# Small 64-row products of two recurrent mixers, regrouped: heads alternate between the halves of the array

## The chip, the cores and the metric

The kernel runs on one core of one Trainium2 chip, in one launch. The metric is the device time of that launch in microseconds (us): the median of three runs of the kernel before is 1320.38 us (1319.36 to 1322.54). About 0.3% (4 us) is what a measurement of this kernel can tell from no change.

## The reference

One layer of a trunk with 256 positions and width 2048: a row norm, one wide projection, two recurrent mixers side by side, an output projection, and a gated feed-forward with its norm and the final norm.

```python
h = rms_norm(x, attn_norm_w);  proj = h @ w_in
y_a = rwkv7_mixer(proj[:, :N_RWKV_IN], ...)      # 16 heads of 64
y_b = gdn_mixer(proj[:, N_RWKV_IN:], ...)        # 8 value heads of 128, 4 key heads
x = x + concat([y_a, y_b]) @ w_out
h = rms_norm(x, ffn_norm_w)
x = x + (silu(h @ w_gate) * (h @ w_up)) @ w_down
out = rms_norm(x, final_norm_w)

# RWKV, one step:   S = S * w_t + (S a_t) b_t^T + v_t k_t^T;   y_t = S r_t
# delta rule, by chunks of 64:
v_new = u_i - w_i @ S                 # u, w: solutions of a unit triangular system of the chunk
o     = qg_i @ S + A_i @ v_new
S     = S * exp(gl_i) + kg_i^T @ v_new
```

Both recurrences are computed in chunks of 64 positions, four chunks for 256 positions. Within a chunk everything is a small matrix product (mostly 64 x 64 or 64 x 128), and the state goes from chunk to chunk.

## The kernel before, in words

**The stream.** Nearly all the work is the product of x (and later of y and of the feed-forward's activations) with weights that come once from memory. A block of weights (128 x 1024) is loaded on SyncE's queue into one of three raw buffers (L167), split by ScalarE into a high part (`wh`, L176) and by VectorE into a low part (`wl`, L177), and used by TensorE in `products` (L198, L199, L200: 128 x 128 weights, 256 columns, three products to a k-block; L195 and L196 in the feed-forward). I call these the stream products. Their result goes to the PSUM tag `pb`.

**The side work.** The mixers are Python generators (`prep`, `chain`, `gdn_v`, `gdn`). After every k-block of the stream `tick()` lets each generator emit its next step when its inputs are there. A scheduler then sets the final order on each engine, and TensorE works strictly through its order: a small product that waits holds the stream products behind it. Three PSUM tags of two banks each serve the side work: `mr` (preparation of RWKV), `mc` (its chain) and `mg` (delta rule).

**The shape of a small product.** The part of the array that a product uses follows from its operands: its rows are the partitions of the two inputs, its columns the partitions of the output. A product with inputs on partitions 0 to 63 and output on partitions 0 to 63 uses one quarter, one with all 128 input partitions and an output on partitions 64 to 127 one half of the columns. The products of full fp32 operands show in the trace as two MATMUL rows each (two passes), so 8 products are "x16" there. Transposes and the stream products show as one.

**RWKV.** Four head pairs p at a time (a half `hf` of the heads). Of the two heads h of a pair one lies on partitions 0 to 63 and one on 64 to 127 (`hr`).
- `prep` makes, per pair, `ps_A` (L464: four chunks for head 0 into one bank, then four for head 1 into another, each bank followed by a masking copy L466).
- `chain` first inverts the triangular blocks, then runs through the chunks: `psR` (L544; heads alternate between the column halves), `psU` (L552; one bank for each head, four pairs each, its copies L553 by ScalarE and by VectorE), `psS` (L561; heads alternate), and `psY`, the output: for each head, per pair, a product with the old state (L580, 64 x 64, not in the first chunk) and then at once one that adds the chunk's own part to it (L581, 128 rows x 64 columns), so the two kinds alternate. One ScalarE copy per head follows (L582).
- After the last chunk the gate: `ps_g`, per pair a product over 128 rows (L617) and one over the remaining 32 rows (L618) of the low-rank input `sgd1`, `sgd2`.

**Delta rule.** `gdn` makes decays and gates, inverts, and runs through four chunks, eight value heads each: `psK` (L856), `psUg` (L867, four heads to a bank, all on the same quarter of the array; copies L871, L873), `psSg` (L881), `psOg` (L895, four heads to a bank, one quarter; copy L896). At the end `ps_og` (L919) transposes the result, L920 scales it into `yg`.

**Where the mixers end.** The output projection multiplies first the half of `w_out` that goes with RWKV's output, then the half that goes with `yg`, which L221 and L222 have split into a high and a low part (`ys`). The delta rule's last chunks run beside the first half.

Of the kernel before, what the change touches and what calls it, by code (L numbers as in the profile page):

```python
# [17 lines left out]
P = 128  # L18
# [31 lines left out]
def trunk_kernel(ctx, tc, xT, vecs, fnw, w_up, a_up, g_up, w_in, w_ab, w_out, w_gu, w_dn, out):  # L50
# [30 lines left out]
    # times a head's rows: less their mean  # L81
    cmat = cp_.tile([P, P], F32, name="cmat")
    V.scalar_tensor_tensor(cmat, bones, -1.0 / 64, ident, ALU.mult, ALU.add)
    # cols 0..63: j < t, cols 64..127: j <= t, with j the partition modulo 64
# [26 lines left out]
    sgd2 = cp_.tile([32, T], F32, name="sgd2")  # L111
# [8 lines left out]
    def rsqrt(y, xh, tag):  # L120
        """1 / sqrt(2 xh) of a few columns of positive numbers: a guess by the exponent, then Newton's steps."""
# [59 lines left out]
    def proj(parts, wide=False, tag="pb"):  # L181
        """parts: [(weight source, rhs tiles)], each of 8 k-blocks of one block of 128 columns."""
        ps = pm.tile([P, 512], F32, tag=tag, name="psb")
        for j, (src, rhs) in enumerate(parts):
            products(ps, load_split(src), rhs, j == 0, j == len(parts) - 1, wide)
        return ps
# [18 lines left out]
    def evac_norm(ps):  # L205
        """an output block of the first projection, times the row norm, to the next of two padded tiles."""
# [29 lines left out]
    # the first blocks of columns: their products with a half of x, while the other comes  # L236
# [29 lines left out]
    # zero, but only when that part of x is split: the squares stand back for the splits  # L266
# [32 lines left out]
    sigmoid(sgd2, pl2[0:32, :])  # L299
# [7 lines left out]
    # 32 x 32 diagonal blocks by forward substitution, a block and every other column of it to a partition  # L307
# [67 lines left out]
    def prep(hf):  # L375
# [15 lines left out]
        for gr in range(2):  # L391
            key = (hf, gr)
            yield lambda: key in kt
            psw, psa = mps("ps_w", "mr"), mps("ps_a", "mr")
# [47 lines left out]
            for pi in range(2):  # L442
# [15 lines left out]
                yield None  # L458
                for h in range(2):
                    hr = slice(h * 64, h * 64 + 64)  # L460
                    ps = mps("ps_A", "mr")
                    ps3 = ps.rearrange("p (c f) -> p c f", c=NCH)
                    for ch in range(NCH):
                        PE.matmul(ps3[:, ch, :], bk[hr, ch].rearrange("p a t -> p (a t)"),  # L464
                                   ar[hr, p, ch].rearrange("p a t -> p (a t)"), start=True, stop=True)
                    V.tensor_tensor(AT[:, h, p], ps3, tmask[:, None, :].to_broadcast([P, NCH, P]), ALU.mult)  # L466
# [8 lines left out]
            # the rows of b make place for a, those of a for the inverse  # L475
# [27 lines left out]
    def chain(hf):  # L503
# [29 lines left out]
        # the output by positions: the norms run along its rows  # L533
# [4 lines left out]
        for ch in range(NCH):  # L538
# [7 lines left out]
            yield None  # L546
            for h in range(2):
                hr = slice(h * 64, h * 64 + 64)
                psU = mps("psU", "mc")
                U3 = psU[0:64, 0:256].rearrange("p (a f) -> p a f", a=4)  # L550
                for p in range(4):
                    PE.matmul(U3[:, p, :], ar[hr, p, ch, 0, :], RR[hr, p, :], start=True, stop=True)  # L552
                (S.copy, V.tensor_copy)[h](UV[0:64, ch, :, hr], U3)  # L553
# [19 lines left out]
            rows = slice(x * 64, x * 64 + 64)  # L573
# [614 lines left out]
```

## Time and profile before

| | |
|---|---|
| runs | 1322.54, 1319.36, 1320.38 us; median 1320.38 |
| span of the profiled execution | 1318.5 us, 1.9 us below the median |
| TensorE busy | 1300.2 us (99%) |
| VectorE busy | 933.2 us (71%) |
| ScalarE busy | 732.0 us (56%) |
| mean granted TensorE clock | 0.995 |
| first to last small product of the mixers (ps_w to ps_og) | 41.1 to about 516 us |
| feed-forward's stream (L195, first start) to the end | from 568.9 us |

The table is read so: TensorE has work nearly all the time. Matmuls overlap in the records (a stream product lasts 0.28 us in its row, but they start every 0.12 us), so what a product costs is seen from the starts of successive rows, not from the duration column.

### The profile page before, as it was taken

To read this page: it belongs to the slowest core of one execution; us is meant where nothing else is said; L and a number is where in the kernel's file an instruction comes from. 1 tells how busy PE (TensorE), PEld (TensorE's weight loads), DVE (VectorE), ACT (ScalarE), POOL (GpSimd) and SP (SyncE) were. 2 spreads that over 40 slices of the span, in tenths; PEclk is the share of its full clock that TensorE was granted. 3 is DMA by queue.
4 is the path that set the end of the run, shared out by engine and by line. 5 is a ranking of instruction groups with operands and counts; after the bars stand their busy time and mean duration, and the time that the engine had idled before them with its cause. 6 is when DMAs were issued, how large, how long until landed. Compare 5 with 4: busy or idle time off the path is not lost.

```text
span 1318.5 us, 23067 instructions
## 1 busy us (share of the span) xinstructions
PE 1300.2 (99%) x8458; PEld 1150.2 (87%) x8458; DVE 933.2 (71%) x1981; ACT 732.0 (56%) x1471; POOL 16.9 (1%) x63
## 2 busy tenths in 40 slices
PE   7999999999999999999999999999999999999997
PEld 7999999898889889998888888888888888888886
DVE  6987798678665667876776666676767676666764
ACT  6666656556644546666655454555555555555553
POOL 1000000000000000000000000000000000000000
PEclk9999999999989999999999999999999999999999
DMA  7454655445546234555765565555555555555541
GB/s 235 146 171 159 165 175 136 129 134 144 130 168 165 90 112 163 195 173 189 256 218 186 190 190 184 193 184 192 190 192 189 186 188 190 191 190 186 187 157 64
DMA packets 108129, 226.80 MB, mean 172 GB/s; under 512 B 52272, under 2 KB 54448, under 8 KB 107760
## 3 DMA queue, kind: packets, MB, share of 16 engines
q1 hardware_dynamic: 103744, 222.19, 53.6%
q10 hardware_dynamic: 4128, 2.10, 0.5%
q8 instruction: 66, 1.08, 0.3%
q0 software_dynamic: 144, 1.05, 0.2%
q14 instruction: 47, 0.39, 0.1%
HBM read 218.75 MB, written 4.46 MB: 169 GB/s over the span
## 4 chain that ended last, share of the span: by engine, by line
PE 96%; DVE 1%; DMA 1%; ACT 0%; issue 0%; SPq 0%; DVEq 0%; ACTq 0%
PE psb L195 25%; PE psd L1055 17%; PE psb L196 12%; PE psb L200 10%; PE psb L199 10%; PE psb L198 10%; PE psY L581 1%; PE ps_A L464 1%; PE psY L580 1%; PE psUg L867 1%; PE psOg L895 1%; DVE wl L177 1%; PE psd L1093 1%; PE psd L1091 1%; PE psd L1092 1%; DMA xraw<-in_xT 1%
## 5 line engine op out<-in xcount | busy, mean ns | idle before, releaser
L176 ACT ACTIVATE wh<-raw 128x512 fp32r<-128x512 f32 x780 | 489.4, 631 | 434.2 <-PE psb L195 139.1
L177 DVE TENSOR_TENSOR wl<-raw,wh 128x512 fp32r<-128x512 f32 x780 | 535.3, 690 | 272.3 <-ACT wh L176 268.3
L195 PE MATMUL psb<-x2s,wh 128*128 128x512 f32 x1408 | 497.4, 398 | 0.0
L196 PE MATMUL psb<-x2s,wl 128*128 128x256 f32 x1408 | 395.1, 282 | 0.7 <-DVE wl L177 0.7
L195 PEld LDWEIGHTS psb<-x2s,wh 128*128 128x128 f32 x1408 | 263.9, 188 | 63.5 <-ACT wh L176 0.2
L196 PEld LDWEIGHTS psb<-x2s,wl 128*128 128x128 f32 x1408 | 265.9, 189 | 3.6 <-DVE wl L177 1.5
L198 PE MATMUL psb<-xs,wh 128*128 128x256 f32 x816 | 236.9, 290 | 8.2 <-ACT wh L176 5.8
L200 PE MATMUL psb<-xs,wl 128*128 128x256 f32 x816 | 237.5, 291 | 0.5 <-DVE wl L177 0.5
L199 PE MATMUL psb<-xs,wh 128*128 128x256 f32 x816 | 237.3, 291 | 0.0
L1055 PE MATMUL psd<-wh,h 128*128 128x512 f32 x640 | 199.2, 389 | 0.0
L198 PEld LDWEIGHTS psb<-xs,wh 128*128 128x128 f32 x816 | 158.5, 194 | 11.5 <-ACT wh L176 5.8
L200 PEld LDWEIGHTS psb<-xs,wl 128*128 128x128 f32 x816 | 158.4, 194 | 5.8 <-issue 2.5
L199 PEld LDWEIGHTS psb<-xs,wh 128*128 128x128 f32 x816 | 158.5, 194 | 3.6 <-issue 1.9
L1055 PEld LDWEIGHTS psd<-wh,h 128*128 128x128 f32 x640 | 119.4, 188 | 24.9
L1055 PE MATMUL psd<-wl,h 128*128 128x512 f32 x320 | 124.4, 389 | 0.0
L200 PE MATMUL psb<-ys,wl 128*128 128x256 f32 x256 | 73.7, 288 | 0.0
L199 PE MATMUL psb<-ys,wh 128*128 128x256 f32 x256 | 73.6, 288 | 0.0
L198 PE MATMUL psb<-ys,wh 128*128 128x256 f32 x256 | 73.3, 286 | 0.0
L1055 PEld LDWEIGHTS psd<-wl,h 128*128 128x128 f32 x320 | 60.1, 188 | 12.5
L1061 DVE TENSOR_TENSOR acc<-acc,psd 128x512 f32<-128x512 f32 x80 | 51.2, 681 | 2.5 <-PE psd L1055 2.5
L200 PEld LDWEIGHTS psb<-ys,wl 128*128 128x128 f32 x256 | 49.0, 191 | 1.6 <-issue 1.5
L199 PEld LDWEIGHTS psb<-ys,wh 128*128 128x128 f32 x256 | 49.0, 191 | 1.5 <-issue 1.4
(315 smaller groups left out, 1152.2 us busy)
## 6 DMA issues: line engine op xcount, KB each, us to landing
raw<-in_w_gu SPq DMA_DIRECT2D x176, 512.0 KB, 3.5
raw<-in_w_in SPq DMA_DIRECT2D x99, 512.0 KB, 3.6
raw<-in_w_dn SPq DMA_DIRECT2D x80, 512.0 KB, 3.5
raw<-in_w_out SPq DMA_DIRECT2D x32, 512.0 KB, 3.6
raw_end<-in_w_dn SPq DMA_DIRECT2D x8, 512.0 KB, 3.9
xraw<-in_xT SPq DMA_DIRECT2D x8, 256.0 KB, 7.5
x<-in_xT SPq DMA_DIRECT2D x1, 2048.0 KB, 8.4
raw<-in_w_ab SPq DMA_DIRECT2D x2, 512.0 KB, 6.9
```

What stands on the lines that cost most here:

```text
L176: S.activation(wh, raw[:, hs], AF.Copy)
L177: V.tensor_tensor(wl, raw[:, hs], wh, ALU.subtract)
L195: PE.matmul(ps, wh[:, ks], rt[:, ri, :], start=st, stop=False)
L196: PE.matmul(ps[:, T:], wl[:, ks], rt[:, ri, 0:T], start=False, stop=sp)
L198: PE.matmul(ps[:, 0:T], wh[:, ks], rt[:, ri, 0:T], start=st, stop=False)
L199: PE.matmul(ps[:, 0:T], wh[:, ks], rt[:, ri, T:], start=False, stop=False)
L200: PE.matmul(ps[:, 0:T], wl[:, ks], rt[:, ri, 0:T], start=False, stop=sp)
L464: PE.matmul(ps3[:, ch, :], bk[hr, ch].rearrange("p a t -> p (a t)"), ar[hr, p, ch].rearrange("p a t -> p (a t)"), start=True, stop=True)
L580: PE.matmul(Y3[rows, p, :], ar[hr, p, ch, 1, :], St[hr, p, :], start=True, stop=False)
L581: PE.matmul(Y3[rows, p, :], AT[:, h, p, ch, 64:128], UV[:, ch, p, hr], start=(ch == 0), stop=True)
L1055: PE.matmul(banks[tb * 2 + cg], st, parts[cg][w], start=(i == 0 and w == 0 and st is hh), stop=(i == n - 1 and st is hl))
L1061: V.tensor_tensor(acc[:, tb, cs], acc[:, tb, cs], banks[tb * 2 + cg], ALU.add)
```

## The change

Seven edits; comments in the source were also dropped, which shifts line numbers by a few.

1. `ps_A`: the two heads' banks are opened together (one from `mr`, one from `mg`), and the products go chunk by chunk, heads alternating. Both masking copies follow the eight products.
2. `psU`: both heads write one bank, each on its own half of the partitions, heads alternating.
3. `psY`: first the eight products with the state, then the eight of the chunk, heads alternating between the halves. The output of a head stands on its own half of the partitions (before: on the half of the chunk's parity). One bank for both heads.
4. `psUg`: one bank for all eight value heads, even heads on partitions 0 to 63, odd ones on 64 to 127, alternating. Its readers take the even and the odd heads apart; VectorE's scaling now stands ahead of ScalarE's copy.
5. `psOg`: the same.
6. `sgd2` and the second part of the gate's weights are padded from 32 to 128 rows with zeros (two memsets on GpSimd), so both products of `ps_g` use all rows.
7. `ps_a` takes its bank from `mg` instead of `mr`.

```diff
-    sgd2 = cp_.tile([32, T], F32, name="sgd2")
+    sgd2 = cp_.tile([P, T], F32, name="sgd2")
+    G.memset(sgd2, 0.0)
...
-            psw, psa = mps("ps_w", "mr"), mps("ps_a", "mr")
+            psw, psa = mps("ps_w", "mr"), mps("ps_a", "mg")
...
+                psA = [mps("ps_A", tg).rearrange("p (c f) -> p c f", c=NCH) for tg in ("mr", "mg")]
+                for ch in range(NCH):
+                    for h in range(2):
+                        hr = slice(h * 64, h * 64 + 64)
+                        PE.matmul(psA[h][:, ch, :], bk[hr, ch].rearrange("p a t -> p (a t)"),
+                                   ar[hr, p, ch].rearrange("p a t -> p (a t)"), start=True, stop=True)
                 for h in range(2):
-                    hr = slice(h * 64, h * 64 + 64)
-                    ps = mps("ps_A", "mr")
-                    ps3 = ps.rearrange("p (c f) -> p c f", c=NCH)
-                    for ch in range(NCH):
-                        PE.matmul(ps3[:, ch, :], bk[hr, ch].rearrange("p a t -> p (a t)"),
-                                   ar[hr, p, ch].rearrange("p a t -> p (a t)"), start=True, stop=True)
-                    V.tensor_tensor(AT[:, h, p], ps3, tmask[:, None, :].to_broadcast([P, NCH, P]), ALU.mult)
+                    V.tensor_tensor(AT[:, h, p], psA[h], tmask[:, None, :].to_broadcast([P, NCH, P]), ALU.mult)
...
+            psU = mps("psU", "mc")
+            U3 = psU[:, 0:256].rearrange("p (a f) -> p a f", a=4)
+            for p in range(4):
+                for h in range(2):
+                    hr = slice(h * 64, h * 64 + 64)
+                    PE.matmul(U3[hr, p, :], ar[hr, p, ch, 0, :], RR[hr, p, :], start=True, stop=True)
             for h in range(2):
                 hr = slice(h * 64, h * 64 + 64)
-                psU = mps("psU", "mc")
-                U3 = psU[0:64, 0:256].rearrange("p (a f) -> p a f", a=4)
-                for p in range(4):
-                    PE.matmul(U3[:, p, :], ar[hr, p, ch, 0, :], RR[hr, p, :], start=True, stop=True)
-                (S.copy, V.tensor_copy)[h](UV[0:64, ch, :, hr], U3)
+                (S.copy, V.tensor_copy)[h](UV[0:64, ch, :, hr], U3[hr])
...
+            psY = mps("psY", "mc")
+            Y3 = psY[:, 0:256].rearrange("p (a f) -> p a f", a=4)
+            ph = [(p, h, slice(h * 64, h * 64 + 64)) for p in range(4) for h in range(2)]
+            if ch:
+                for p, h, hr in ph:
+                    PE.matmul(Y3[hr, p, :], ar[hr, p, ch, 1, :], St[hr, p, :], start=(p == 0), stop=False)
+            for p, h, hr in ph:
+                PE.matmul(Y3[hr, p, :], AT[:, h, p, ch, 64:128], UV[:, ch, p, hr], start=(ch == 0 and p == 0),
+                           stop=(p == 3))
             for h in range(2):
-                hr = slice(h * 64, h * 64 + 64)
-                psY = mps("psY", "mc")
-                Y3 = psY[:, 0:256].rearrange("p (a f) -> p a f", a=4)
-                for p in range(4):
-                    if ch:
-                        PE.matmul(Y3[rows, p, :], ar[hr, p, ch, 1, :], St[hr, p, :], start=True, stop=False)
-                    PE.matmul(Y3[rows, p, :], AT[:, h, p, ch, 64:128], UV[:, ch, p, hr], start=(ch == 0), stop=True)
-                S.copy(Yt[rows, cp, :].rearrange("p (a h f) -> p h a f", a=4, h=2)[:, h], Y3[rows])
+                S.copy(Yt[rows, cp, :].rearrange("p (a h f) -> p h a f", a=4, h=2)[:, h], Y3[h * 64:h * 64 + 64])
...
-        lg, lg2 = yl[:, 1024:1536], yl[0:32, 1536:2048]
+        lg, lg2 = yl[:, 1024:1536], yl[:, 1536:2048]
+        G.memset(lg2, 0.0)
         SY.dma_start(out=lg, in_=g_up[0:128, cs])
-        SY.dma_start(out=lg2, in_=g_up[128:160, cs])
+        SY.dma_start(out=lg2[0:32, :], in_=g_up[128:160, cs])
...
-            for i in range(2):
-                psU = mps("psUg", "mg")
-                for j in range(4):
-                    h = 4 * i + j
-                    PE.matmul(psU[rows, j * P:j * P + P], TT[rows, 2 * h + cp, :], vn[rows, cp, h, :],
-                               start=True, stop=True)
-                u3 = psU.rearrange("p (h f) -> p h f", h=4)
-                hs = slice(4 * i, 4 * i + 4)
-                S.copy(vn[rows, cp, hs, :], u3[rows])
-                if ch < NCH - 1:
-                    V.tensor_tensor(vs[rows, hs, :], u3[rows],
-                                     GT[rows, cp, hs][:, :, None].to_broadcast([64, 4, P]), ALU.mult)
+            psU = mps("psUg", "mg")
+            u3 = psU.rearrange("p (h f) -> p h f", h=4)
+            for h in range(8):
+                PE.matmul(u3[h % 2 * 64:h % 2 * 64 + 64, h // 2, :], TT[rows, 2 * h + cp, :], vn[rows, cp, h, :],
+                           start=True, stop=True)
+            if ch < NCH - 1:
+                for m in range(2):
+                    V.tensor_tensor(vs[rows, m::2, :], u3[m * 64:m * 64 + 64],
+                                     GT[rows, cp, m:8:2][:, :, None].to_broadcast([64, 4, P]), ALU.mult)
+            for m in range(2):
+                S.copy(vn[rows, cp, m::2, :], u3[m * 64:m * 64 + 64])
...
+            psO = mps("psOg", "mg")
+            o3 = psO.rearrange("p (h f) -> p h f", h=4)
+            for h in range(8):
+                PE.matmul(o3[h % 2 * 64:h % 2 * 64 + 64, h // 2, :], gam[rows, h, cp, :], vn[rows, cp, h, :],
+                           start=True, stop=True)
+            for m in range(2):
+                S.activation(vn[rows, cp, m::2, :], o3[m * 64:m * 64 + 64], AF.Copy, scale=-1.0)
```

How the order on TensorE changes is shown at two places. The first is a later chunk of RWKV's first half: `psY` behind the last of `psS`, where `St` is the old state, `ar` and `AT` the chunk's operands. A row "x7" stands for seven products in succession. Before, the first two pairs of the first head:

```order
L561 MATMUL psS<-UV_484,bkn_483 64x64 x7
L580 MATMUL psY<-St_1792,ar_481 64x64
L581 MATMUL psY<-UV_484,AT_482 64x64
L580 MATMUL psY<-St_1792,ar_481 64x64
L581 MATMUL psY<-UV_484,AT_482 64x64
```

The two kinds go on in turn to the fourth pair, and the second head follows later in the same way.

Now, both heads (L583 and L585 are the former L580 and L581):

```order
L564 MATMUL psS<-UV_485,bkn_484 64x64 x7
L583 MATMUL psY<-St_1792,ar_482 64x64 x8
L585 MATMUL psY<-UV_485,AT_483 64x64 x8
L200 MATMUL psb<-xs_145,wh 128x256
L201 MATMUL psb<-xs_145,wl 128x256
```

The sixteen products of a chunk stood in sixteen separate stretches of one kind, and stand in two.

The second place is the end of the delta rule: the last transposes (`ps_og`) and the first product of the output projection that reads its result (`ys_5950` before, `ys_5929` now). Before, the last four transposes stand 52 stream products ahead of that product; the rows just ahead of it and the product itself are these:

```order
L198 MATMUL psb_6501<-ys_5947,wh_6508 128x256
L199 MATMUL psb_6501<-ys_5947,wh_6508 128x256
L200 MATMUL psb_6501<-ys_5947,wl_6509 128x256
L198 MATMUL psb_6537<-ys_5950,wh_6540 128x256
L199 MATMUL psb_6537<-ys_5950,wh_6540 128x256
```

Now the last eight transposes stand directly ahead of it:

```order
L201 MATMUL psb_6480<-ys_5926,wl_6488 128x256
L924 MATMUL ps_og_5782<-ident_71,vnknSg_3713 128x128 x4
L924 MATMUL ps_og_5915<-ident_71,vnknSg_3713 128x128 x4
L199 MATMUL psb_6516<-ys_5929,wh_6519 128x256
L199 MATMUL psb_6555<-ys_5929,wh_6558 128x256
```

Between the last transposes and the first reader of the delta rule's result stood 52 stream products, and stand none.

More of the change, by code (lines that the diff above doesn't have):

```diff
@@ L298, in trunk_kernel @@
     pr = evac_shift(ps_first[2], VEC["mu_l"] + 2, pl2)
-    sigmoid(sgd2, pl2[0:32, :])
+    sigmoid(sgd2[0:32, :], pl2[0:32, :])
     ra, rb = slice(32, 40), slice(64, 72)
@@ L889, in gdn @@
                                                     psS[:, j * P:j * P + P], ALU.mult, ALU.add)
-            for i in range(2):
-                psO = mps("psOg", "mg")
-                for j in range(4):
-                    h = 4 * i + j
-                    PE.matmul(psO[rq, j * P:j * P + P], gam[rows, h, cp, :], vn[rows, cp, h, :], start=True, stop=True)
-                S.activation(vn[rows, cp, 4 * i:4 * i + 4, :].rearrange("p h f -> p (h f)"), psO[rq], AF.Copy, scale=-1.0)
-                if ch == 0:
-                    continue
-                for j in range(4):
-                    h = 4 * i + j
-                    V.scalar_tensor_tensor(vn[rows, cp, h, :], psK[i][rq, j * P:j * P + P], GTn[rq, cp, h:h + 1],
-                                            vn[rows, cp, h, :], ALU.mult, ALU.add)
+            psO = mps("psOg", "mg")
[5 more added lines that the diff above has]
+                S.activation(vn[rows, cp, m::2, :], o3[m * 64:m * 64 + 64], AF.Copy, scale=-1.0)
+            for h in range(8 if ch else 0):
+                V.scalar_tensor_tensor(vn[rows, cp, h, :], psK[h // 4][rq, h % 4 * P:h % 4 * P + P],
+                                        GTn[rq, cp, h:h + 1], vn[rows, cp, h, :], ALU.mult, ALU.add)
             if x:
```

## The prediction

> **What bounds the kernel now.** I read the page first: the busy line and the chain of work that ended last.
>
> ```profile
> span 1318.5 us, 23067 instructions
> PE 1300.2 (99%) x8458; PEld 1150.2 (87%) x8458; DVE 933.2 (71%) x1981; ACT 732.0 (56%) x1471; POOL 16.9 (1%) x63
> PE 96%; DVE 1%; DMA 1%; ACT 0%; issue 0%; SPq 0%; DVEq 0%; ACTq 0%
> ```
>
> TensorE is the chain, from start to end. The list of TensorE's waits has only one entry for a small product:
>
> ```profile
> PE psS L561 <- DVE UV L553: 1.1, 1, 1.1
> ```
>
> So between 40 and 516 us, where the mixers run beside the stream, every microsecond that a small product holds TensorE is a microsecond of the kernel, as long as its inputs stay early. The question is what the small products hold, and that is read in the timeline of TensorE, from start to start. I measure a stretch of small products so: from the start of the last stream product ahead of it to the start of the second stream product behind it (the first one still starts late), less 0.12 us for each stream product in between, since stream products start every 0.12 us (247.71 to 247.83 here). The first stretch is `psR`, eight products, whose heads already alternate between the halves of the columns:
>
> ```profile
> 247.71 0.28 PE L200 MATMUL psb<-xs,wl 128*128 128x256 f32 x1
> 247.83 0.28 PE L198 MATMUL psb<-xs,wh 128*128 128x256 f32 x1
> 248.04 0.69 PE L544 MATMUL psR<-UV,AT 128*64 128x64 f32 x16
> 248.88 0.28 PE L200 MATMUL psb<-xs,wl 128*128 128x256 f32 x1
> ```
>
> That is 1.05 - 0.24 = 0.81 us for 16 passes. `psU`, eight products of the same size in which one head's four come first, is next:
>
> ```profile
> 251.63 0.28 PE L199 MATMUL psb<-xs,wh 128*128 128x256 f32 x1
> 251.84 0.96 PE L552 MATMUL psU<-RR,ar 64*64 64x64 f32 x16
> 252.95 0.28 PE L198 MATMUL psb<-xs,wh 128*128 128x256 f32 x1
> ```
>
> It holds 1.32 - 0.24 = 1.08 us. And `psY`, one head, in which two shapes (64 x 64 and 128 x 64) alternate:
>
> ```profile
> 244.52 0.28 PE L198 MATMUL psb<-xs,wh 128*128 128x256 f32 x1
> 244.72 0.33 PE L580 MATMUL psY<-St,ar 64*64 64x64 f32 x2
> 244.98 0.33 PE L581 MATMUL psY<-UV,AT 128*64 128x64 f32 x2
> ...
> 247.00 0.28 PE L200 MATMUL psb<-xs,wl 128*128 128x256 f32 x1
> ```
>
> It holds 2.48 - 0.24 = 2.24 us for the same 16 passes. So two things cost: every change of shape, and products that follow each other on the same part of the array.
>
> **The price of a change of shape** comes from the delta rule, where four products of `psOg` stand in one stretch and four of the same size of `psUg` in two, one stream product apart:
>
> ```profile
> 452.17 0.28 PE L198 MATMUL psb<-xs,wh 128*128 128x256 f32 x1
> 452.38 1.08 PE L895 MATMUL psOg<-vnknSg,gates 64*64 64x128 f32 x8
> 453.62 0.28 PE L200 MATMUL psb<-xs,wl 128*128 128x256 f32 x1
> ```
>
> ```profile
> 462.98 0.28 PE L200 MATMUL psb<-ys,wl 128*128 128x256 f32 x1
> 463.18 0.43 PE L867 MATMUL psUg<-vnknSg,TTg 64*64 64x128 f32 x2
> 463.54 0.38 PE L198 MATMUL psb<-ys,wh 128*128 128x256 f32 x1
> 463.86 0.86 PE L867 MATMUL psUg<-vnknSg,TTg 64*64 64x128 f32 x6
> 464.87 0.28 PE L200 MATMUL psb<-ys,wl 128*128 128x256 f32 x1
> ```
>
> One stretch: 1.45 - 0.24 = 1.21 us. Two: 1.89 - 0.36 = 1.53 us. So going out of the stream's shape and back costs 0.32 us, whatever stands in between; what remains of the 1.21 us is 0.89 us for 8 passes, 0.11 us each. In the same way `psR` is 0.81 - 0.32 = 0.49 us of work for 16 passes, 0.03 us a pass.
>
> **The change part by part.**
>
> *psY.* Before: in the three later chunks of both halves, 12 head stretches of 2.24 us, 26.9 us. In the first chunk only L581: half of `psU`'s passes, (1.08 - 0.32) / 2 + 0.32 = 0.70 us, four times, 2.8 us. Now a later chunk has two stretches of 16 passes that alternate; each is a `psR`. They stand next to each other, so the second adds its work and one change: a change between shapes costs what L580 to L581 shows, 0.26 us for two passes of (1.08 - 0.32) / 16 = 0.05 us, so 0.16 us. Together 0.81 + 0.49 + 0.16 = 1.46 us, six times 8.8 us. The first chunks: 0.81 twice, 1.6 us. The order splits L585 in one place of each half (1 and 7 products, standing apart from L583): about 0.5 us more each, 1.0 us. Gain 29.7 - 11.4 = 18.3 us.
>
> *ps_A.* Eight stretches of eight products, 64 rows x 128 columns, one head after the other:
>
> ```profile
> 83.71 0.28 PE L199 MATMUL psb<-xs,wh 128*128 128x256 f32 x1
> 83.92 1.71 PE L464 MATMUL ps_A<-ar,bk 64*128 64x128 f32 x16
> 85.78 0.28 PE L198 MATMUL psb<-xs,wh 128*128 128x256 f32 x1
> ```
>
> That is 2.07 - 0.24 = 1.83 us. If the heads run beside each other, eight pairs of passes at 0.11 us take 0.88 us, and with 0.32 to 0.40 us for the changes about 1.25 us. Gain 0.58 x 8 = 4.6 us; two of the stretches were split in the order of before, 0.6 us more. 5.2 us.
>
> *psU.* 1.08 becomes 0.81 us, eight times, 2.2 us; two stretches were split, 0.6 us. Together 2.8 us.
>
> *psOg.* 8 stretches of 1.21 us become 4 that hold twice the products in the same 1.21 us, if two run beside each other; one of them is split (0.32 us). 9.7 - 5.2 = 4.5 us.
>
> *psUg.* In the order its 32 products stood in 23 stretches and stand in 15: 8 x 0.32 = 2.6 us. Within the new stretches 12 pairs can run beside each other, each saving two passes, 12 x 0.22 = 2.6 us. 5.2 us.
>
> *ps_g.* Two pairs of products, of which every second one uses only 32 rows:
>
> ```profile
> 279.49 0.28 PE L200 MATMUL psb<-xs,wl 128*128 128x256 f32 x1
> 279.61 0.59 PE L617 MATMUL ps_g<-sgd,yl 128*128 128x256 f32 x2
> 280.13 0.69 PE L618 MATMUL ps_g<-sgd,yl 32*128 32x256 f32 x2
> 282.23 0.28 PE L199 MATMUL psb<-xs,wh 128*128 128x256 f32 x1
> ```
>
> They hold 2.74 - 0.24 = 2.50 us for 8 passes. The full shape costs what `psK` of the same size costs for 4 passes:
>
> ```profile
> 461.52 0.28 PE L198 MATMUL psb<-ys,wh 128*128 128x256 f32 x1
> 461.64 1.02 PE L856 MATMUL psK<-vnknSg,kq 128*128 128x256 f32 x4
> 462.62 0.28 PE L200 MATMUL psb<-ys,wl 128*128 128x256 f32 x1
> ```
>
> 1.10 - 0.24 = 0.86 us, so 8 passes take 1.72 us. Gain 0.78 x 4 = 3.1 us. The zeros behind it cost two memsets on GpSimd (1% busy), the second ahead of a load on SyncE's queue; 40 and 48 stream products stand ahead of the first `ps_g`, about 5 us of cover.
>
> *ps_a's bank* moves two products and gains nothing: in the order `ps_w` and `ps_a` of the later groups still stand apart. Sum on TensorE: 18.3 + 5.2 + 2.8 + 4.5 + 5.2 + 3.1 = 39.1 us.
>
> **The clock.** Twice the granted clock was low in this stage:
>
> ```profile
> 349.00:353.00 4.00, 4.00 (x23) 3.88 (x23) 2.94 (x12) 2.33 (x7) 0.00 (x0) 0.61 0.34 119
> 382.00:389.00 7.00, 7.00 (x38) 6.23 (x38) 1.78 (x7) 3.38 (x13) 0.00 (x0) 0.56 0.44 147
> ```
>
> The column is the one ahead of the DMA share: 0.61 and 0.56 cost 4 x 0.39 + 7 x 0.44 = 4.6 us. Both follow on `psY` and `psS` with little array in use for microseconds, which the change makes short. I take 3 us of the 4.6 as gone (0 to 4.6). The Trainium skill ("TensorE: Matmul & The Clock Gate", Part 1) says that the clock is halved after a window of about 3.4 us in which TensorE was idle. In the second window TensorE's row is busy all 7.00 us, so by that rule taken literally the change would not touch it, and the forecast would be some 3 us higher.
>
> **What comes back.** The order puts the last eight `ps_og` directly ahead of the first reader of `yg`. Behind the transposes come the scaling on VectorE and the split:
>
> ```profile
> 513.39 1.05 ACT L221 ACTIVATE ys<-vnknSg 128x1024 fp32r<-128x1024 f32 x1
> 515.22 1.21 DVE L222 TENSOR_TENSOR ys<-vnknSg,ys 128x1024 fp32r<-128x1024 f32 x1
> 512.00:517.00 5.00, 5.00 (x45) 5.00 (x45) 5.00 (x9) 2.66 (x5) 0.00 (x0) 1.00 0.58 168
> ```
>
> VectorE is busy 5.00 of 5.00 us there, so the split stands in a queue. In-order TensorE, with all stream products behind it, then waits: 1.05 + 1.21 us if the queue is empty, about twice that if two stream splits stand ahead, less what the transposes and 24 products of the first half of `ys` cover. I take 4 us, 1 to 7 as bounds.
>
> Elsewhere the cover looks kept. `psU`'s later copy, and the rest of `psS` that needs it:
>
> ```profile
> 253.14 0.41 DVE L553 COPY UV<-psU 64x256 f32<-64x256 f32 x1
> 256.49 0.68 PE L561 MATMUL psS<-UV,bkn 128*64 128x64 f32 x14
> ```
>
> 2.9 us lie between. Now both copies wait for the whole of `psU` (0.3 us later for the first one), but the order puts 13 to 23 stream products between `psU` and `psS` (19 here before), 1.6 to 2.8 us, and `psU` itself is 0.3 us shorter. Taken at nothing.
>
> **The sum.** -39.1 - 3 + 4 = -38.1 us: the span goes from 1318.5 to 1280.4 us, and with the 1.9 us between span and median, 1320.4 to 1282.3 us.
>
> **The rivals.**
>
> A. *Heads in opposite halves do not run beside each other when they write one bank.* `psR` shows it for halves of the columns with the same rows. `psU` and the state products of `psY` use opposite rows and columns at once and write one bank; no row of before shows that. If they run one after the other, 14 stretches of 16 passes cost 16 x 0.05 + 0.32 = 1.12 instead of 0.81 us: 4.3 us back, 1287 us. The Trainium skill ("TensorEngine Tiling (Array Packing)", Gotcha 1) states that different row tiles cannot access the same PSUM bank at the same time; it is this rule that speaks against the change. Chance 0.12.
>
> B. *The delta rule's chain becomes the bound.* TensorE reaches its end 39 us earlier, while VectorE's and ScalarE's part of the chain is as long as before and VectorE is already full there. Then the 9.7 us gained in `psUg` and `psOg`, and some of the clock's, turn into waits ahead of the second half of the projection: 1290 to 1296 us. Against it: the order's distances between the steps of the chain grew (32 stream products from `psUg` to `psSg`, 3 to 13 before). Chance 0.13.
>
> C. *No new pair overlaps, only the changes of shape are saved.* Then `psU` gains 0.6, `ps_A` 0.6, `psOg` 4 x 0.32 - 0.32 = 1.0, `psUg` 2.6, `ps_g` 3.1, and `psY` 29.7 - (6 x (2 x 1.08 - 0.16) + 2 x 1.08 + 1) = 14.5 us: 22 us, so 1299 us with the rest as above. `psR`'s row speaks against it. Chance 0.04.
>
> D. *Slower.* Eight products now share a bank, so their readers start only behind the eighth, and the next product of the chain behind the readers. Where `psUg` stood in two fours, the first four were read while the second four ran. There are 24 such steps (8 `psU`, 8 `psY`, 4 `psUg`, 4 `psOg`). If each lost its cover of about 2.5 us, 60 us would come, 1342 us; it decides above 38 / 24 = 1.6 us a step. The distances in the order speak against it. Chance 0.03.
>
> **How the numbers follow.** The forecast, 1282 us, has 0.66; its own range is 1276 (both low clocks gone, wait of 1 us, somewhat more pairs) to 1289 (clock as before, wait of 7 us). A and B lie at 1287 to 1296. The range 1275 to 1296 holds the forecast, A and B and leaves out C, D and the ends. No change (within 0.3%, which is what a measurement of this kernel can tell) has 0.02, as no case of mine ends there. Faster: 0.66 + 0.12 + 0.13 + 0.04 = 0.95. Slower: 0.03.
>
> **What would show each step.** In the profile after, `psU` and both kinds of `psY` should have stretches of 0.8 us as `psR` has, `ps_A` 1.25 us, `psOg` 1.2 us with x16; a stretch of `psU` over 1.05 us is A. The low clock should be gone between 330 and 390 us. The waits should list the split of `ys` (L222, L223 now) with some 4 us; over 8 us is B. Waits of over 1 us ahead of `psS`, `psSg` or `psK` are D. The feed-forward's 750 us should be as before; if they differ by more than 1 us, my whole account misses something.

## The result, and the profile after

| | before | after |
|---|---|---|
| median, runs beside each other | 1319.87 us (4 runs) | 1284.42 us (1281.59 to 1289.42, 4 runs) |
| ratio | | 0.9729 (95% interval 0.9702 to 0.9756) |
| time and span of the profiled execution | 1320.4, 1318.5 us | 1289.4, 1287.7 us |
| start of the feed-forward's stream | 568.9 us | 536.8 us |

The profiled execution is the longest of the four. The changed kernel was run in two more sessions; its 13 executions have a mean of 1284.2 us (standard error 0.7), the 42 of the kernel before that ran beside the experiments 1320.5 us (0.3). So the change takes 36.3 us off.

The page of the changed kernel, its span, the busy line and the shares of the chain that ended last:

```profile
span 1287.7 us, 23086 instructions
PE 1264.9 (98%) x8458; PEld 1127.3 (88%) x8458; DVE 930.3 (72%) x1981; ACT 726.7 (56%) x1469; POOL 18.1 (1%) x66
PE 91%; DMA 4%; DVE 2%; ACT 1%; SPq 1%; issue 0%; DVEq 0%; ACTq 0%
```

TensorE lost 35.3 us of busy time, and its share of the chain fell from 96 to 91%: transfers, their queue, VectorE and ScalarE now stand in it for 8%, where they had 2%.

The stretches themselves, from the timeline of TensorE. `psU`, and a later chunk's `psY` (both heads):

```profile
241.77 0.28 PE L201 MATMUL psb<-xs,wl 128*128 128x256 f32 x1
241.98 0.68 PE L553 MATMUL psU<-RR,ar 64*64 64x64 f32 x16
242.59 0.39 PE L199 MATMUL psb<-xs,wh 128*128 128x256 f32 x1
242.81 0.28 PE L200 MATMUL psb<-xs,wh 128*128 128x256 f32 x1
...
231.88 0.68 PE L583 MATMUL psY<-St,ar 64*64 64x64 f32 x16
232.50 0.69 PE L585 MATMUL psY<-UV,AT 128*64 128x64 f32 x16
233.11 0.39 PE L200 MATMUL psb<-xs,wh 128*128 128x256 f32 x1
```

`psU` holds 1.04 - 0.24 = 0.80 us (1.08 before). `psY`'s 32 passes hold 1.23 us from their first start (231.88) to the next stream product (233.11). Measured in the same way, the 16 passes of one head held 2.06 us before (the 2.24 us of the prediction count from the stream product ahead). `psOg`, now all eight heads:

```profile
427.93 0.28 PE L201 MATMUL psb<-ys,wl 128*128 128x256 f32 x1
428.13 1.09 PE L901 MATMUL psOg<-vnknSg,gates 64*64 64x128 f32 x16
429.16 0.39 PE L199 MATMUL psb<-ys,wh 128*128 128x256 f32 x1
429.38 0.28 PE L200 MATMUL psb<-ys,wh 128*128 128x256 f32 x1
```

1.45 - 0.24 = 1.21 us for 16 passes, what 8 passes cost before.

The list of TensorE's waits has entries that were not there before:

```profile
PE psb L199 <- ACT wh L177: 6.3, 1, 6.3
PE psF_g L351 <- DMA Bd_g<-sG: 2.2, 1, 2.2
PE psb L201 <- DVE wl L178: 1.7, 3, 0.8
PE psF_r L351 <- DMA ar<-sX_r: 1.6, 1, 1.6
PE psb L197 <- DVE wl L178: 1.5, 3, 0.6
PE psb L200 <- DVE ys L223: 1.3, 2, 0.8
PE psb L199 <- ACT ys L222: 0.3, 1, 0.3
```

The first is the start of the kernel, as before. The two of `psF` belong to the block inverse: `psF_r` to RWKV's first half, `psF_g` to the delta rule. The waits on `ys` are the ones forecast. And the clock, in stretches cut where the granted clock changes (columns: from and to, length, busy time of the five engines, clock, DMA share, GB/s):

```profile
200.85:204.26 3.41, 1.81 (x17) 1.64 (x16) 3.38 (x8) 0.98 (x2) 0.00 (x0) 1.00 0.94 162
204.27:207.68 3.41, 3.41 (x18) 3.41 (x18) 2.26 (x6) 1.52 (x3) 0.00 (x0) 0.50 0.58 231
381.76:385.17 3.41, 1.19 (x11) 1.01 (x10) 1.76 (x4) 1.22 (x2) 0.00 (x0) 1.00 0.77 197
385.18:392.01 6.83, 6.83 (x34) 6.83 (x34) 2.22 (x4) 1.41 (x4) 0.00 (x0) 0.50 0.88 251
```

The half clock is not gone: it stands in two other places, each directly behind 3.41 us in which TensorE was busy for only 1.81 and 1.19 us, because it waited ahead of `psF`.

**Term by term.** I summed the same measure over all stretches of both traces (from each product's start to the next start, plus what the neighbouring stream products start late):

| | before | after | gain | forecast |
|---|---|---|---|---|
| psY | 29.4 | 10.2 | 19.3 | 18.3 |
| ps_A | 15.3 | 9.4 | 5.9 | 5.2 |
| psU | 9.1 | 7.0 | 2.1 | 2.8 |
| psOg | 9.3 | 5.2 | 4.2 | 4.5 |
| psUg | 14.6 | 9.4 | 5.2 | 5.2 |
| ps_g | 10.0 | 6.9 | 3.1 | 3.1 |
| sum | | | 39.7 | 39.1 |
| psF, its wait included | 5.4 | 11.6 | -6.2 | 0 |

About 1.0 us of `psY`'s gain is half clock that lay on it before. `psF` is the one large entry that the forecast did not have; 1.6 of its 6.2 us are half clock, and in the other two profiled executions of the changed kernel it is 8.1 and 8.3 us (-2.7 and -2.9). The feed-forward takes 750.9 us to the end in this execution, 1.3 us more than before (749.6), and so more than the 1 us that the prediction named as a sign that its account misses something. In the other two it takes 749.8 and 749.0 us, on both sides of the value before, so this is spread between executions and not an effect of the change.

### The profile page after: what moved, and what is told of

Same layout as the page of the kernel before. It is cut to its first block, busy times and chain, and to the rows that moved or that the text cites. A ratio compares the mean times of both kernels' runs of the same rounds, so it can differ in the third digit from the quotient of the medians.

```text
span 1287.7 us, 23086 instructions
## 1 busy us (share of the span) xinstructions
PE 1264.9 (98%) x8458; PEld 1127.3 (88%) x8458; DVE 930.3 (72%) x1981; ACT 726.7 (56%) x1469; POOL 18.1 (1%) x66
## 3 DMA queue, kind: packets, MB, share of 16 engines
q8 instruction: 66, 1.08, 0.3%
## 4 chain that ended last, share of the span: by engine, by line
PE 91%; DMA 4%; DVE 2%; ACT 1%; SPq 1%; issue 0%; DVEq 0%; ACTq 0%
PE psb L196 23%; PE psd L1060 17%; PE psb L197 12%; PE psb L201 10%; PE psb L200 9%; PE psb L199 9%; DMA raw_end<-in_w_dn 2%; PE ps_A L464 1%; DVE wl L178 1%; PE psd L1098 1%; PE psd L1096 1%; PE psd L1097 1%; PE psUg L874 1%; DMA raw<-in_w_gu 1%; PE psSg L888 0%; DVE wend L178 0%
## 5 line engine op out<-in xcount | busy, mean ns | idle before, releaser
L200 PEld LDWEIGHTS psb<-ys,wh 128*128 128x128 f32 x256 | 49.0, 191 | 2.8 <-DVE ys L223 1.7
L199 PEld LDWEIGHTS psb<-ys,wh 128*128 128x128 f32 x256 | 48.8, 191 | 1.8 <-issue 1.2
```

The source lines that it names most:

```text
L199: PE.matmul(ps[:, 0:T], wh[:, ks], rt[:, ri, 0:T], start=st, stop=False)
L200: PE.matmul(ps[:, 0:T], wh[:, ks], rt[:, ri, T:], start=False, stop=False)
```

## The experiments

The theory after the result: the gain is the sum of the forecast's terms, partly from fewer changes of shape and partly from products running beside each other, and a few microseconds come back because TensorE now arrives at the block inverse before it is ready. Rivals: grouping alone makes the gain (C); `psY`'s gain is mostly the clock; the delta rule's chain is the bound (B).

**1. psY alone.** The kernel before, with this edit only:

```diff
+            psY = mps("psY", "mc")
...
+            if ch:
+                for p, h, hr in ph:
+                    PE.matmul(Y3[hr, p, :], ar[hr, p, ch, 1, :], St[hr, p, :], start=(p == 0), stop=False)
+            for p, h, hr in ph:
+                PE.matmul(Y3[hr, p, :], AT[:, h, p, ch, 64:128], UV[:, ch, p, hr], start=(ch == 0 and p == 0),
+                           stop=(p == 3))
...
-                for p in range(4):
-                    if ch:
-                        PE.matmul(Y3[rows, p, :], ar[hr, p, ch, 1, :], St[hr, p, :], start=True, stop=False)
-                    PE.matmul(Y3[rows, p, :], AT[:, h, p, ch, 64:128], UV[:, ch, p, hr], start=(ch == 0), stop=True)
...
```

> The kernel before with the psY edit alone (one bank, heads on their own halves, first the eight products with the state, then the eight of the chunk). My sum gives psY 18.3 us of the 39.1, without any of the other edits and without the end of the delta rule moving: about 1302 us (1299 to 1305), ratio 0.986. If psY's gain were mostly the low clock near 350 and 385 us going away, the time would fall by over 21 us. Rival A (no overlap of opposite rows and columns in one bank) gives about 14.5 us of gain: 1305 us, with stretches of psY's state products over 1.05 us.

Measured: 1296.86 us, ratio 0.9823 (0.9807 to 0.9840), 23.5 us faster. That is more than the 18.3 us of `psY`'s products: the time lies below the expected 1299 to 1305 us, and the gain is over the 21 us that I had named for a gain that is mostly the clock. The windows of the trace say how much of it is the clock. Of this kernel, the two stretches that had 0.61 and 0.56 before, and the whole region:

```profile
349.00:353.00 4.00, 4.00 (x63) 3.46 (x63) 4.00 (x17) 1.53 (x3) 0.00 (x0) 1.00 0.41 141
382.00:389.00 7.00, 6.98 (x47) 5.48 (x46) 2.73 (x6) 2.28 (x4) 0.00 (x0) 1.00 0.87 213
330.00:400.00 70.00, 69.20 (x667) 63.49 (x665) 52.82 (x160) 38.05 (x99) 1.91 (x2) 1.00 0.60 184
```

The clock is full throughout. The mean granted clock of its four executions is 0.9978 against 0.9942 in 42 of the kernel before; over 1320 us that is 4.7 us. In the traces `psY` falls from 29.4 to 9.3 us, of which 1.0 was half clock: 19.1 + 4.7 = 23.8 us. So four fifths are the stretches, as forecast, and the clock is the smaller part, though larger than the 3 us that I had taken.

**2. Everything but psY.** The changed kernel with the old `psY` put back:

```diff
-            psY = mps("psY", "mc")
...
-            if ch:
-                for p, h, hr in ph:
-                    PE.matmul(Y3[hr, p, :], ar[hr, p, ch, 1, :], St[hr, p, :], start=(p == 0), stop=False)
...
+                psY = mps("psY", "mc")
...
+                for p in range(4):
+                    if ch:
+                        PE.matmul(Y3[rows, p, :], ar[hr, p, ch, 1, :], St[hr, p, :], start=True, stop=False)
...
```

> The changed kernel with psY as it was before. By my sum the other edits gain 20.8 us on TensorE; less some 2 to 7 us of new waits seen in the changed kernel: 1301 to 1306 us. If the terms add up, this gain and that of psY alone together make the gain of the whole change (35 us at the median); if the edits share a cost (the same waits and low clocks), the two differ from it by over 4 us.

Measured: 1301.97 us (1298.86 to 1305.95), ratio 0.9861 (0.9836 to 0.9887), 18.4 us faster. The two gains together, 41.8 us, are 5.5 us more than that of the whole change: the second branch of the expectation. The whole change has a cost that neither part has alone: the list of waits of the first kernel has no `psF` at all, the second's has 0.2 us. The trace of the second kernel also shows the clock most clearly, in two stretches of 3.41 us, and the first and last of the `psY` rows that fill the first one:

```profile
355.66:359.07 3.41, 3.41 (x28) 2.46 (x26) 1.61 (x5) 0.37 (x1) 0.00 (x0) 1.00 0.46 154
359.08:362.49 3.41, 3.41 (x18) 3.17 (x17) 0.60 (x2) 2.17 (x8) 0.53 (x1) 0.50 0.51 127
```

```profile
355.74 0.33 PE L585 MATMUL psY<-UV,AT 128*64 128x64 f32 x2
356.00 0.32 PE L584 MATMUL psY<-St,ar 64*64 64x64 f32 x2
...
359.08 0.47 PE L584 MATMUL psY<-St,ar 64*64 64x64 f32 x2
```

TensorE's row is busy for 3.41 of 3.41 us, nothing waits, and the clock is halved right behind it: in this execution no idling was needed, and small products that alternate in kind filled the stretch.

**3. Same groups, heads one after the other.** The changed kernel, with the same banks and readers:

```diff
-                for ch in range(NCH):
-                    for h in range(2):
+                for h in range(2):
+                    for ch in range(NCH):
...
-            ph = [(p, h, slice(h * 64, h * 64 + 64)) for p in range(4) for h in range(2)]
+            ph = [(p, h, slice(h * 64, h * 64 + 64)) for h in range(2) for p in range(4)]
...
-            for h in range(8):
+            for h in (0, 2, 4, 6, 1, 3, 5, 7):
```

(`psU` as `ps_A`; `psUg` and `psOg` both as the last.)

> The changed kernel with every new group kept together (same banks, same readers, same number of changes of shape), but within a group one head's products follow each other on the same part of the array and then the other's (psA, psU, both kinds of psY, psUg, psOg). If half of the gain is two products running beside each other, as my account of starts says: psY 6 x 2 x 0.27 + 2 x 0.27 = 3.8, psU 2.2, psA 4.6, psUg up to 2.6, psOg 4 x 0.85 = 3.4, in all about 16 us slower than the changed kernel, 1298 to 1302 us. If grouping alone does it (rival C: only changes of shape cost), it stays within 3 us of the changed kernel, 1284 to 1287 us.

Measured: 1292.67 us, ratio 0.9791 (0.9776 to 0.9805): 8.6 us slower than the mean of the changed kernel. Rival C falls, but the 16 us were too many. `psU` here:

```profile
224.71 0.28 PE L201 MATMUL psb<-xs,wl 128*128 128x256 f32 x1
224.92 0.96 PE L553 MATMUL psU<-RR,ar 64*64 64x64 f32 x16
225.81 0.39 PE L199 MATMUL psb<-xs,wh 128*128 128x256 f32 x1
226.04 0.28 PE L200 MATMUL psb<-xs,wh 128*128 128x256 f32 x1
```

1.33 - 0.24 = 1.09 us, as before the change; that it writes one bank changes nothing, and alternating the heads is worth 0.29 us. Summed over the stretches the difference to the changed kernel is 10.7 us (`ps_A` 4.6, `psY` 2.5, `psU` 1.7, `psOg` 1.4, `psUg` 0.6). `psOg` was mis-sized most (3.4 expected): in the trace's single records the second group of heads starts its first four passes beside the last four of the first group, so a group in sequence is not without overlap. And 2 us or more came off `psF` (6.1 us here, 8.1 to 11.6 in the changed kernel), at which TensorE arrived later. Of the changed kernel's 39.7 us the alternation of heads is therefore some 11; grouping, with the overlap that it brings by itself, is the rest, some 29.

**4. psY's two kinds in turn again,** heads still alternating:

```diff
-            if ch:
-                for p, h, hr in ph:
...
-            for p, h, hr in ph:
...
+            for q in range(4):
+                if ch:
+                    for p, h, hr in ph[2 * q:2 * q + 2]:
...
+                for p, h, hr in ph[2 * q:2 * q + 2]:
...
```

(The products' `start` and `stop` flags are again those of the kernel before.)

> The changed kernel, but psY's two kinds alternate pair by pair again (state product of both heads, then the chunk's of both heads), with heads still alternating between the halves. Six chunks get 7 changes between shapes in place of 1. At 0.16 us a change, as I worked it out: 6 x 6 x 0.16 = 5.8 us slower than the changed kernel, 1290 us. If a change between these two shapes costs nothing by itself and only products on the same part of the array cost, within 1 us of it.

Measured: 1289.23 us, ratio 0.9765 (0.9750 to 0.9780), 4.8 us above the changed kernel's first median and 5.2 us above its mean. The first and the last rows of one chunk:

```profile
233.03 0.33 PE L584 MATMUL psY<-St,ar 64*64 64x64 f32 x4
233.29 0.34 PE L586 MATMUL psY<-UV,AT 128*64 128x64 f32 x4
...
234.87 0.34 PE L586 MATMUL psY<-UV,AT 128*64 128x64 f32 x4
235.14 0.39 PE L200 MATMUL psb<-xs,wh 128*128 128x256 f32 x1
```

2.11 us where the changed kernel has 1.23: 0.88 us for six more changes, 0.15 us each. The price of a change between shapes (0.16 us in the forecast) holds. A rival would be that a chunk's product costs because it adds to an output that its partner wrote just before, here 0.26 us earlier. The changed kernel's single records speak against it: there the partner started 0.61 us earlier, and the one change between the kinds costs the same 0.15 us.

**5 and 6. The wait ahead of psF_g.** `psF_g` has two inputs: `Bd_g`, a block matrix that comes in eight loads on SyncE's queue behind a memset on GpSimd, and `tn_g`, the substitution's result, which goes out to memory, comes back (`st_g`) and is transposed on VectorE. In the changed kernel's timeline, first VectorE: the last step of the substitution and that transpose.

```profile
372.15 0.18 DVE L327 TENSOR_TENSOR X_g<-X_g,tmp_g 128x16 f32<-128x16 f32 x1
380.97 0.45 DVE L346 STREAM_TRANSPOSE tn_g<-st_g 128x256 f32<-128x256 f32 x1 [3.31 <-DMA st_g<-sX_g]
```

Then GpSimd's memset, which could start only when the substitution no longer read the old content of that buffer, the first and the last of the loads on SyncE's queue, and TensorE:

```profile
371.68 0.96 POOL L338 MEMSET Bd_g<- 128x1024 f32 x1 [22.85 <-DMA raw<-in_w_in]
...
373.68 2.37 SPq L837 DMA_DIRECT2D Bd_g<-sG  x3
...
381.12 1.83 SPq L837 DMA_DIRECT2D Bd_g<-sG  x3
...
384.97 3.40 PE L351 MATMUL psF_g<-tn_g,Bd_g 128*128 128x32 f32 x16 [2.22 <-DMA Bd_g<-sG]
```

The loads are last: issued until 382.95 us, and the product starts 2.0 us behind that.

I gave `Bd_g` another buffer and issued its loads ahead of the substitution; in the changed kernel (5) and, as a control, in the kernel before (6):

```diff
         load_blocks(A)
+        if nm == "g":
+            Bd = ip.tile([P, 2, 8, P], F32, tag="bkn1", name=f"Bd_{nm}")[:, 0]
+            G.memset(Bd, 0.0)
+            load_bd(Bd)
...
-        Bd = ip.tile([P, 8, P], F32, tag="i1", name=f"Bd_{nm}")
-        G.memset(Bd, 0.0)
-        load_bd(Bd)
+        if nm != "g":
+            Bd = ip.tile([P, 8, P], F32, tag="i1", name=f"Bd_{nm}")
+            G.memset(Bd, 0.0)
+            load_bd(Bd)
```

> The changed kernel, but the delta rule's block matrix Bd gets a buffer of its own, so its memset and its eight loads are issued ahead of the substitution and not behind the release of the old buffer at 372 us. If the wait ahead of psF at 382 us (2.5 us) comes from those late loads, and the 6.8 us of half clock that follow it come from the wait: the wait goes, and with it some 3.4 us of clock, 2.2 to 6 us faster than the changed kernel. Rival: the low clock does not hang on this wait and comes anyway somewhere in this stretch: at most 2.2 us faster, with a low-clock window still between 340 and 400 us.

> Control: the same edit on the kernel before, which has no wait ahead of psF at that place but has two low-clock windows, at 349 and 383 us. Expected: no difference (within 1.5 us of the kernel before); if it gains over 2 us, the edit does something other than take away the wait that the change brought.

Measured: 1281.97 us, ratio 0.9706 (0.9693 to 0.9718); the control 1319.11 us, ratio 0.9985 (0.9974 to 0.9995). The wait on `Bd_g` is gone and no low clock was left before the end in the profiled execution. But the control gained some 2 us as well (2.1 us on the mean of the runs beside it, standard error 0.6), where it had no such wait, and that is just over the 2 us that I had named as a sign that the edit does something else. So the comparison was made again beside the changed kernel.

> The changed kernel once more, beside the next two on one chip, so that they can be compared: 1282 to 1287 us. If low clock follows the waits ahead of psF (theory), executions differ by how many windows of 3.41 us fall wholly into such a wait: a spread of some 7 us, lower mean clock with longer time.

> Bd early, once more, for a close comparison. Theory (the late loads of Bd cost their wait of 2.2 us and some of the low clock): 2 to 5 us faster than the changed kernel beside it, with a mean clock nearer 0.998 (only the window behind TensorE's last work is left) and a smaller spread. Rival (the first comparison was chance): within 1.5 us.

Measured: 1282.52 us for the changed kernel, 1282.09 us with the loads early, ratios 0.9716 (0.9693 to 0.9739) and 0.9704 (0.9680 to 0.9728): the rival's branch. The waits and the windows of that second execution with early loads show why:

```profile
PE psF_g L356 <- DVE tn_g L351: 1.3, 1, 1.3
```

```profile
377.44:380.85 3.41, 2.08 (x18) 1.88 (x18) 1.29 (x3) 1.26 (x2) 0.01 (x1) 1.00 0.88 172
380.86:387.68 6.82, 6.82 (x34) 6.82 (x34) 2.78 (x6) 2.01 (x4) 0.00 (x0) 0.50 0.78 223
```

The loads are no longer last, but now the other input, `tn_g`, is: TensorE is there at 378.6 us, and the transpose ends at 380.0 us. The half clock behind the wait came with it. The edit did more than I had meant: it also changed the order on TensorE. The traces have 2273 stream products ahead of `psF_g` in the changed kernel and 2255 with the loads early, so the product stands 18 of them, some 2.2 us, earlier. In the changed kernel above the transpose had ended at 381.4 us, before TensorE came to the product at 382.6 us. At the old place here TensorE would have come at some 380.7 us (378.6 + 18 x 0.12, an estimate), and `tn_g` would have been ready.

Over all executions (9 against 13) the loads early are 2.1 us faster (standard error 1.0), no more than the control gained. So the wait on `Bd_g` did come from the late loads, but what its removal brings by itself is not shown.

**7. The delta rule's two edits taken out.** The changed kernel with `psUg` and `psOg` as before:

```diff
-            psU = mps("psUg", "mg")
...
-            for h in range(8):
-                PE.matmul(u3[h % 2 * 64:h % 2 * 64 + 64, h // 2, :], TT[rows, 2 * h + cp, :], vn[rows, cp, h, :],
-                           start=True, stop=True)
...
+            for i in range(2):
+                psU = mps("psUg", "mg")
+                for j in range(4):
+                    h = 4 * i + j
+                    PE.matmul(psU[rows, j * P:j * P + P], TT[rows, 2 * h + cp, :], vn[rows, cp, h, :],
+                               start=True, stop=True)
...
```

(`psOg` in the same way, and the readers with them.)

> The changed kernel with psUg and psOg as they were before. My sum: 5.2 + 4.5 = 9.7 us slower than the changed kernel on TensorE, about 1294 us, less what of the wait at the end of the delta rule (2 to 2.4 us at ys) goes: 1291 to 1295 us. Rival B (VectorE's and ScalarE's part of the chain is the bound there, so TensorE's gain in psUg and psOg only became waiting): at most 2 us slower, 1284 to 1286 us.

Measured: 1292.06 us, ratio 0.9786 (0.9768 to 0.9804), 7.8 us above the changed kernel's mean (standard error 1.5). Rival B falls: TensorE's gain there was not swallowed. In the stretches the two edits are worth 10.2 us (`psUg` 15.2 to 9.4, `psOg` 9.5 to 5.2). The list of waits has no `ys` here (1.6 us in the changed kernel), which fits the 2.4 us between 10.2 and 7.8: some 2 us of the gain had been given back at the delta rule's end.

**8. The wait ahead of ys.** Loads early, and the split of the delta rule's result in pieces of two heads:

```diff
-        split(t[:, :, 0:T], t[:, :, T:], src)
+        for e in range(2) if len(ys) > 1 else (slice(0, 4),):
+            e = slice(2 * e, 2 * e + 2) if isinstance(e, int) else e
+            split(t[:, e, 0:T], t[:, e, T:], src[:, e])
```

> Bd early, and the split of the delta rule's result into ys made in pieces of two heads (four of 0.6 us on each engine in place of two of 1.05 and 1.21), so that 24 stream products of the projection's second half stand between the last transposes and their first reader of heads 4 to 7. Theory (the end of the delta rule costs the 2.0 to 2.4 us seen ahead of L199 and L200, and nothing more hangs on it): 1.5 to 2.5 us faster than Bd early alone. Rival B in a weak form (VectorE's queue there is the bound, the wait only moves to a later reader): within 1 us.

Measured beside the two runs above (1282.52 and 1282.09 us): 1279.51 us, ratio 0.9695 (0.9669 to 0.9722). That is 2.6 us below the loads early alone by the medians and 2.2 us by the means (standard error 1.9), about as expected, but too close to the noise to rule out the rival's 1 us. In the list of waits the one on L222 is gone and the other is down:

```profile
PE psb L200 <- DVE ys L223: 0.8, 1, 0.8
```

Once more, against the changed kernel on one chip:

> The changed kernel a third time, for the comparison with the next: 1282 to 1284 us.

> Bd early and the split of ys in halves, against the changed kernel beside it. If both waits count (ahead of psF at 382 us some 1 us on balance, ahead of ys some 1.5 us): 2 to 4 us faster, 1279 to 1281 us. If each wait only moves to the next link: within 1 us.

Measured: 1285.89 us and 1282.05 us, ratios 0.9732 (0.9706 to 0.9759) and 0.9701 (0.9677 to 0.9725). Both lie above what I expected, the changed kernel by 1.9 us and the other by 1.1 us; the difference, 3.8 us, is as expected. Over both sessions (10 executions, mean 1280.5 us, standard error 0.9) this kernel is 3.7 us below the changed one (1.1 for the difference), and has the lowest mean of all that were run. Against the loads early alone it is 1.5 us lower (1.1), so what the split of `ys` brings by itself is not settled.

## Why the prediction was right, point by point

- **The forecast, 1282 us (1275 to 1296), against 1284.4.** Right in sign, in size and in the main mechanism. That it came so close owes something to luck: the wait at the end was put some 2 us too high, and the one ahead of `psF`, 2 to 5 us at full clock, was not in the sum.
- **The terms.** Their sum, 39.1, measured 39.7 us; none is off by more than 1.0. The method, from start to start, did it: by durations `psY`'s row would have given 34.8 us of work before (18.9 + 15.9 in the groups), where it held 29.4. The price of a change of shape holds by itself (experiment 4). That of products side by side holds where two groups alternate in full (`psU` 0.29 us against 0.27), but the split within other terms was off: `psUg`'s 5.2 us were forecast as 2.6 from fewer stretches and 2.6 from pairs, and by experiment 3 alternating the heads is worth only 0.6 of them; of `psOg`'s 4.2 it is 1.4, where 3.4 had been expected. These terms came out right as sums, not in their parts.
- **Rival A.** `psU` at 0.80 us refutes it: opposite rows and columns overlap as well as columns alone, in one bank. The rule of the Trainium skill ("TensorEngine Tiling (Array Packing)", Gotcha 1), that different row tiles cannot access one PSUM bank at the same time, does not agree with this trace: the products of the two heads use different rows, write one bank, and start 6 to 7 ns apart in the single records of `psU`.
- **Rivals B and C** fell in experiments 7 and 3, though what C counts on, grouping, is the larger part of the gain (some 29 of 39.7 us). **D**: no wait of over 0.1 us ahead of `psS`, `psSg` or `psK`; the cover taken at nothing was there.
- **The clock, -3 us.** The size is right on the mean: 0.9964 over 13 executions against 0.9942, 1320 x 0.0022 = 2.9 us. The step behind it was half right. That `psY` no longer brings the clock down is shown (experiments 1 and 2); that the low clock would then be gone between 330 and 390 us was wrong: in the changed kernel waits ahead of `psF` bring it back in some executions. `psY` alone gained 4.7 us of clock in experiment 1, as much as the 4.6 us of the two windows. So the 2.9 us look like a larger gain less what those waits took, and that my 3 us met them is partly luck. As in experiment 2, a low clock of the kernel before follows a window in which TensorE's row was busy all the time:

```profile
379.42:382.83 3.41, 3.41 (x29) 2.54 (x27) 2.27 (x7) 0.87 (x2) 0.00 (x0) 1.00 0.52 154
382.84:389.67 6.83, 6.83 (x34) 6.26 (x34) 1.87 (x6) 3.01 (x12) 0.00 (x0) 0.50 0.54 185
```

  So the rule taken literally (the Trainium skill, "TensorE: Matmul & The Clock Gate", Part 1: half clock after an idle window of about 3.4 us) misses this one and the one of experiment 2. Its window length agrees (3.41 us); in these two the row was not idle.
- **The wait at the end, +4 us.** The place is right (L222, L223), the size was over: 1.6 us in the list of waits, and some 2 us by experiment 7 (2.4, standard error 1.5).
- **What failed: "Elsewhere the cover looks kept."** I had followed what the edits themselves touch. The block inverse is not touched, but its substitution runs on VectorE, then through two transfers, at a pace that TensorE's gain shortens only in part. In the profile of before, the transpose, the last loads of `Bd_g` and the product stood so:

```profile
407.63 0.45 DVE L345 STREAM_TRANSPOSE tn_g<-st_g 128x256 f32<-128x256 f32 x1 [2.14 <-DMA st_g<-sX_g]
404.29 3.48 SPq L830 DMA_DIRECT2D Bd_g<-sG  x3
410.35 1.87 PE L350 MATMUL psF_g<-tn_g,Bd_g 128*128 128x32 f32 x16
```

  The product started 2.3 us behind the transpose's end; the last load, issued at 407.2 us and landing in some 2.4 us (the median of the eight), left some 0.7 us. TensorE then arrived 28 us earlier, while the substitution ended only 24 us earlier (at 372.3 us against 396.6). Both products `psF` together, with their waits, cost 2.7 and 2.9 us more in two profiled executions and 6.2 us, with half clock, in the third. Some 0.5 to 2.2 us of this are `psF_r`'s, at which no experiment was aimed.
- **The balance:** 38.7 (terms without their half clock) + 2.9 (clock) - 2 (`ys`) - 2.2 to 4.6 (`psF` at full clock, in three profiled executions) = 35.0 to 37.4 us; measured 36.3.

Left open: why the early loads bring the kernel before some 2 us too, and whether these are the clock's. Its mean is 0.9949 there over 12 executions against 0.9942, about 1 us; nothing else was tried on it.

## What to carry to other kernels

Where small products share a stream with large ones, count starts, not durations: here each change of the array's shape had a price (0.15 us), and products on different parts of the array ran beside each other when they stood next to each other in the order. Put products of one shape together and alternate their halves. When TensorE gets ahead by tens of microseconds, look up how much cover every chain on other engines has, also of steps that the change does not touch, and for each wait ask which other input arrives next. An edit that moves a load can move products too: compare the order on TensorE before you put a difference down to the load.

## What the runs showed that I had not expected

- **Half clock without idling.** It began behind 3.41 us of alternating small products with TensorE's row busy for all 3.41 us (at 382.84 us before, at 359.08 us in experiment 2).
- **A fixed grid.** Wherever a profiled execution has several starts of low clock, they lie whole multiples of 3.413 us apart: 348.71 and 382.84 us before are 10 steps, 204.27 and 385.18 us after 53. Which stretch fills a whole step differs by execution, so the same wait is followed by half clock in one and not in another: 1.9 us ahead of `psF_g` in experiment 7 left the clock full. No sharp limit of array use was found that tells the steps apart.
- **Overlap across a seam.** Products of one half in sequence, then of the other half, overlapped for four passes where the groups meet (`psOg` and `psU` in experiment 3, and already `psU` of the kernel before).
